# Expert gates of two dense blocks: one-hot products, or indirect additions into a zeroed DRAM tensor

## The chip, the cores and the metric

The kernel runs on one core of one Trainium2 chip, as one launch. Its metric is device time in microseconds, of three runs the median: 1672.23 (1667.02 to 1674.17). One further execution was taken by the hardware profiler; all rows of a profile here are from it. Engine names in rows: PE is TensorE, PEld its weight loads, DVE VectorE, ACT ScalarE, POOL GpSimd, SP SyncE, which issues nearly all plain transfers.

## The reference

One layer of a decoder trunk for 512 tokens of width 1024, fp32: a token-mixing half (attention over a window of 128, causal pooling, gated merge, residual), then PEER, a retrieval over 128 x 128 experts, then RMSNorm. The change lies in PEER, which per token is:

```python
q  = (xc @ w_query).reshape(c, 8, 2, 128)               # 8 heads, two halves
sc = einsum('chpd,hpkd->chpk', q, sub_keys)
sv, si = top_k(sc, 16)                                  # top 16 of 128 keys per half
cand = sv[:, :, 0, :, None] + sv[:, :, 1, None, :]      # 256 candidates
cidx = si[:, :, 0, :, None] * 128 + si[:, :, 1, None, :]
fv, fi = top_k(cand, 16);  idx = take_along_axis(cidx, fi)
g = softmax(fv)
a = gelu(einsum('chkd,cd->chk', u_tab[idx], xc))
out = einsum('chk,chkd->cd', g * a, v_tab[idx])         # 8 x 16 experts a token
```

Two heads of a token may choose the same expert, and then their gates add up; one head never chooses an expert twice.

## The kernel before

The 512 tokens are four blocks of 128. Block 0 goes ahead alone, with its tokens' experts fetched row by row from the tables (`gather`: 128 fetches of U rows and 128 of V rows, each an indirect transfer of GpSimd that brings one 4 KB row per token into one of five row buffers; VectorE multiplies by one instruction a fetch, L906 and L910). Blocks 1 to 3 are computed densely against all 16384 experts on the U side: 128 **U parts**, one per value of the expert's upper index i, each 24 matmuls of 128 x 128 by 384 columns (three products for split precision), whose Gelu gives, for the 128 lower indices j, the activations of the three blocks. Block 1's go to DRAM (`late`) and are picked from there one by one; those of blocks 2 and 3, 256 tokens, are kept in SBUF (`gk`, as many as `HELD` and `KEEP` allow) or written to DRAM (`ahead`) and reloaded. After the U parts comes the **dense stage**: for each i the activations are multiplied by a gate tile [j, token] (`mix`), split in two, and multiplied with the 128 V rows of that i (`v_mm`), while block 1's V rows are fetched by GpSimd (`gather_late`).

The gate tile is a dense matrix over experts and tokens with 128 nonzeros a token. Before, `onehot` makes it token by token: from the chosen experts' i, j and gates, transposed, ScalarE builds relu(g - g|j - j'|) (`absolute`, L746, and `build`, L752), VectorE the comparison of i (L755), TensorE one fp32 product of the two per token (L764, two instructions each), ScalarE copies eight tokens out of PSUM (L765), and SP writes 1 MB for each 16 tokens to `spill` (L767). `gate_tile` (L811) reads it back in four transfers of 256 KB for eight values of i, in runs of 512 B.

What sets the order: `run` (L941) issues parts one after another and between two of them spends a credit on a queue of background work. That queue is: choose the experts of block 2 (`select`, VectorE), of block 3, spread block 2, choose block 1, spread block 3, at a credit of `R_A` = 3.8 a part; beside it the fetches of block 0, at a rate that ends them four parts before the last. VectorE also splits each part's weights (L121), in its own program order between the products of fetched rows and the background's instructions. GpSimd does nothing here but issue indirect transfers, in order; a fetch waits for a free row buffer, which a product on VectorE frees.

Of the kernel before, what the change touches and what calls it, by code (L numbers as in the profile page):

```python
# [19 lines left out]
P = 128  # L20
# [26 lines left out]
TG = 16  # L47
NG = TD // TG
AJ = 4
NI = 8  # L50
# [4 lines left out]
HP = 400  # L55
U_S = 4
LOOK = 2
KEEP = 4
HELD = (42, 50)
# [4 lines left out]
class Layer:  # L64
    def __init__(self, ctx, tc, a):
        self.ctx, self.tc, self.nc, self.a = ctx, tc, tc.nc, a
        nc = self.nc
        self.c = self.pool("const", 1)
        self.s = self.pool("small", 2)
        self.w = self.pool("wstream", 2)  # L70
        self.rows = self.pool("rows", ROWS, side="right", reuse_waits="tile")
        self.work, self.owed = [], 0.0
# [17 lines left out]
        self.spill = nc.dram_tensor("spill", (NG, P, NKEY, TG), F32, kind="Internal").ap()  # L90

    def consts(self):
# [6 lines left out]
        self.tok = self.c.tile([P, 1], I32, name="tok")  # L99
# [522 lines left out]
    def scores(self, xn2, tp, sv, si, subk):  # L622
# [23 lines left out]
        for i in range(16):  # L646
# [10 lines left out]
            yield  # L657
        match(i, last)
# [60 lines left out]
    def indices(self, tp, ei):  # L719
        v = self.nc.vector  # L720
        ij = tp.tile([P, 2, P], I32, name="ij", tag="ij", bufs=1)
        v.tensor_scalar(ij[:, 0, :], ei, 7, None, op0=ALU.arith_shift_right)
        v.tensor_scalar(ij[:, 1, :], ei, NKEY - 1, None, op0=ALU.bitwise_and)
        jf = tp.tile([P, 2, P], F32, name="jf", tag="jf", bufs=2)
        v.tensor_copy(jf[:, 0, :], ij[:, 0, :])
        v.tensor_scalar(jf[:, 1, :], ij[:, 1, :], -1.0, None, op0=ALU.mult)
        return jf

    def onehot(self, tp, c, jf, g):
        nc = self.nc  # L730
        v = nc.vector
        ps = self.mm_tile(3 * P)
        for n, src in enumerate((jf[:, 0, :], jf[:, 1, :], g)):
            nc.tensor.transpose(ps[:, n * P:(n + 1) * P], src, self.ident)
        yield 2
        tr = tp.tile([P, 4, P], F32, name="tr3", tag="tr3", bufs=1)
        v.tensor_copy(tr[:, :3, :].rearrange("p a b -> p (a b)"), ps)
        v.tensor_scalar(tr[:, 3, :], ps[:, 2 * P:], -1.0, None, op0=ALU.mult)
        iob = self.iota.unsqueeze(1).to_broadcast([P, 8, P])
        gs = {}  # L740

        def absolute(n):
            u = 8 * n
            ohj = tp.tile([P, 8, P], F32, name="ohj", tag="k4", bufs=4)
            for z in range(8):
                nc.scalar.activation(ohj[:, z, :], self.iota, AF.Abs, bias=tr[:, 1, u + z:u + z + 1])  # L746
            return ohj

        def build(n, ohj):
            u = 8 * n  # L750
            for z in range(8):
                nc.scalar.activation(ohj[:, z, :], ohj[:, z, :], AF.Relu, bias=tr[:, 2, u + z:u + z + 1],  # L752
                                     scale=tr[:, 3, u + z:u + z + 1])
            ohi = tp.tile([P, 8, P], F32, name="ohi", tag="k4", bufs=4)
            v.tensor_tensor(ohi, iob, tr[:, 0, u:u + 8].unsqueeze(2).to_broadcast([P, 8, P]), op=ALU.is_equal)  # L755
            return ohj, ohi

        def product(n, ohj, ohi):
            t0 = 8 * n % TG
            if t0 == 0:  # L760
                gs[0] = tp.tile([P, NKEY, TG], F32, name="gs", tag="gs", bufs=2)
            pg = self.big([P, 8, P], "pg")
            for z in range(8):
                nc.tensor.matmul(pg[:, z, :], lhsT=ohj[:, z, :], rhs=ohi[:, z, :], start=True, stop=True)  # L764
            nc.scalar.copy(gs[0][:, :, t0:t0 + 8].rearrange("p i t -> p t i"), pg)  # L765
            if t0 + 8 == TG:
                nc.sync.dma_start(out=self.spill[(c * P + 8 * n) // TG], in_=gs[0])  # L767

        last = None
        for n in range(P // 8):  # L770
            ohj = absolute(n)
            yield 2.4
            new = build(n, ohj)
            yield 3.2
            if last:
                product(n - 1, *last)
                yield 1.9
            last = new
        product(n, *last)
# [26 lines left out]
    def gate_tile(self, n, q, parts=4):  # L806
        b = n // NI
        if q == 0:
            self.gts[b] = self.dp.tile([P, NG, NI, TG], F32, name="gt", tag="gt", bufs=2)
        s = slice(q * NG // parts, (q + 1) * NG // parts)  # L810
        self.nc.sync.dma_start(out=self.gts[b][:, s].rearrange("p g i t -> p g (i t)"),  # L811
                               in_=self.spill[s, :, n:n + NI, :].rearrange("g p i t -> p g (i t)"))

# [8 lines left out]
    def mix(self, m):  # L822
        nc, dp, gts = self.nc, self.dp, self.gts
        ga = self.reload(m)
        if 0 < m % NI < 5 and m - m % NI + NI < NKEY:
            self.gate_tile(m - m % NI + NI, m % NI - 1)
# [3 lines left out]
        nc.vector.tensor_tensor(wf.rearrange("p (g t) -> p g t", t=TG), ga.rearrange("p (g t) -> p g t", t=TG),  # L830
                                gts[m // NI][:, :, m % NI, :], op=ALU.mult)
# [39 lines left out]
    def rows_of(self, tab, ei, s):  # L871
        t = self.rows.tile([P, D], F32, name="row", tag="row")
        self.nc.gpsimd.indirect_dma_start(out=t, out_offset=None, in_=tab,  # L873
                                          in_offset=bass.IndirectOffsetOnAxis(ap=ei[:, s:s + 1], axis=0))
        return t

    def gather_late(self, ei, ea, g, z):
# [3 lines left out]
        def elem(s):  # L881
            nc.gpsimd.indirect_dma_start(out=act[:, s:s + 1], out_offset=None, in_=self.late,  # L882
                                         in_offset=bass.IndirectOffsetOnAxis(ap=ea[:, s:s + 1], axis=0))
# [57 lines left out]
    def run(self):  # L941
# [12 lines left out]
        with tc.tile_pool(name="route", bufs=1, side="right", reuse_waits="tile") as tp:  # L954

            def pool(b):
                return self.ga if b == LB else tp

# [3 lines left out]
            def wide(shape):  # L962
                return tp.tile(shape, F32, name="eq", tag="k4", bufs=4)
# [4 lines left out]
            ei = {b: pool(b).tile([P, P], I32, name=f"ei{b}", bufs=1) for b in late_blocks}  # L968
            gw = {b: pool(b).tile([P, P], F32, name=f"gw{b}", bufs=1) for b in late_blocks}
            ea = self.ga.tile([P, P], I32, name="ea", bufs=1)  # L970

            jf = {}

            def choose(b):
                yield from self.select(small, wide, sv[b], si[b], ei[b], gw[b])
                if b >= VB:
                    jf[b] = self.indices(tp, ei[b])
                else:
                    nc.vector.tensor_scalar(ea, ei[b], 7, None, op0=ALU.logical_shift_left)
                    nc.vector.tensor_tensor(ea, ea, self.tok.to_broadcast([P, P]), op=ALU.bitwise_or)  # L980
                yield 1

            def spread(b):
                yield from self.onehot(tp, b - VB, jf[b], gw[b])
# [20 lines left out]
            bg = Background(choose(2), choose(3), spread(2), choose(LB), spread(3))  # L1005
            rate = (2 * PH * TOPK - fetch.spent) / (NKEY - ahead - 4)
            while not bg.done:
                after = part()
                with tc.issue_after(after):
                    bg.spend(R_A)  # L1010
                    fetch.spend(rate)
        self.home, self.room = self.pool("more", 1, reuse_waits="tile"), HELD[1]
        while ahead < NKEY:
            with tc.issue_after(part()):
                fetch.spend(rate)
        fetch.spend(1e9)
        self.xs.close()
        with tc.tile_pool(name="dense", bufs=2, reuse_waits="tile") as self.dp:
# [7 lines left out]
            late = Background(self.gather_late(ei[LB], ea, gw[LB], h1))  # L1026
# [34 lines left out]

def blocks(w):
# [42 lines left out]
```

## Time and profile before

| | us |
|---|---|
| runs, median (lowest to highest) | 1672.23 (1667.02 to 1674.17) |
| the profiled execution | 1678.03 |
| its span, first to last instruction | 1676.0 |
| TensorE busy, and share | 1515.9, 90% |
| VectorE | 1276.3, 76% |
| ScalarE | 835.7, 50% |
| GpSimd | 668.8, 40% |
| mean granted TensorE clock | 0.961 |

The span is what the trace shows; the profiled execution's own time lies 2 us above it. Shares are means over stages that differ: mixing and block 0 up to about 500 us, scores of blocks 1 to 3 up to about 600, U parts up to 1200, the dense stage after that. A matmul's length in a row is that of its passage through a pipeline; matmuls start closer to each other than they are long, so the pace of TensorE is read from their count in a stretch. A GpSimd row with DMA_INDIRECT is the time GpSimd needs to issue the transfer, not the transfer's.

### The profile page before, as it was taken

To read this page: it belongs to the slowest core of one execution; us is meant where nothing else is said; L and a number is where in the kernel's file an instruction comes from. 1 tells how busy PE (TensorE), PEld (TensorE's weight loads), DVE (VectorE), ACT (ScalarE), POOL (GpSimd) and SP (SyncE) were. 2 spreads that over 40 slices of the span, in tenths; PEclk is the share of its full clock that TensorE was granted. 3 is DMA by queue.
4 is the path that set the end of the run, shared out by engine and by line. 5 is a ranking of instruction groups with operands and counts; after the bars stand their busy time and mean duration, and the time that the engine had idled before them with its cause. 6 is when DMAs were issued, how large, how long until landed. Compare 5 with 4: busy or idle time off the path is not lost.

```text
span 1676.0 us, 23878 instructions
## 1 busy us (share of the span) xinstructions
PE 1515.9 (90%) x8234; PEld 1356.9 (81%) x8234; DVE 1276.3 (76%) x2395; ACT 835.7 (50%) x1663; POOL 668.8 (40%) x518
## 2 busy tenths in 40 slices
PE   6898979999779989789999999999789898888887
PEld 5797967899679979789999999999766665666665
DVE  2402878889857999977789876677379898898898
ACT  4411346643234333399994999833334343333344
POOL 0000010255520024544435544354277776676730
PEclk9998989999889999989999999999899999999999
DMA  7685242499973348789999999998689999999995
GB/s 270 229 296 206 70 162 94 161 349 341 363 263 105 129 157 295 258 289 344 334 356 316 381 354 345 360 323 313 188 278 357 357 343 369 358 376 372 347 358 206
DMA packets 189465, 476.41 MB, mean 284 GB/s; under 512 B 21408, under 2 KB 84896, under 8 KB 187040
## 3 DMA queue, kind: packets, MB, share of 16 engines
q1 hardware_dynamic: 128736, 270.31, 45.5%
q0 software_dynamic: 59392, 201.42, 34.1%
q10 hardware_dynamic: 1216, 3.15, 0.6%
q8 instruction: 65, 1.06, 0.3%
q14 instruction: 56, 0.46, 0.1%
HBM read 438.50 MB, written 35.78 MB: 283 GB/s over the span
## 4 chain that ended last, share of the span: by engine, by line
PE 28%; DMA 10%; ACT 9%; DVE 7%; issue 4%; POOL 1%; DVEq 0%; ACTq 0%; POOLq 0%
DMA wr<-v_experts 8%; PE mm L116 6%; PE mm L117 6%; PE mm L118 6%; DVE wl L121 4%; PE acc L117 4%; PE acc L118 3%; PE acc L116 3%; ACT wh L127 2%; ACT ohj L752 2%; ACT ohj L746 2%; PE pg L764 2%; ACT gs L765 1%; POOL act L882 1%; DVE h L895 1%
## 5 line engine op out<-in xcount | busy, mean ns | idle before, releaser
L121 DVE TENSOR_TENSOR wl<-wr,wh 128x1024 fp32r<-128x1024 f32 x315 | 385.5, 1225 | 199.0 <-ACT wh L127 196.7
L116 PE MATMUL mm<-xh,wh 128*128 128x384 f32 (+1 forms) x1408 | 486.3, 346 | 19.1 <-ACT gk L795 16.6
L127 ACT CAST wh<-wr 128x1024 fp32r<-128x1024 f32 x315 | 331.9, 1054 | 331.6 <-PE mm L117 239.0
L118 PE MATMUL mm<-xh,wl 128*128 128x384 f32 (+1 forms) x1408 | 479.7, 341 | 7.3 <-DVE wl L121 7.3
L117 PE MATMUL mm<-xl,wh 128*128 128x384 f32 (+1 forms) x1408 | 479.0, 340 | 5.6 <-DVE xl L121 5.6
L873 POOL DMA_INDIRECT row<-u_experts,eig x128 | 196.8, 1537 | 602.6 <-DVE hg L910 250.7
L116 PEld LDWEIGHTS mm<-xh,wh 128*128 128x128 f32 x1408 | 267.8, 190 | 27.1 <-ACT gk L795 19.4
L118 PEld LDWEIGHTS mm<-xh,wl 128*128 128x128 f32 x1408 | 267.7, 190 | 8.8 <-DVE wl L121 8.8
L117 PEld LDWEIGHTS mm<-xl,wh 128*128 128x128 f32 x1408 | 267.7, 190 | 6.0 <-DVE xl L121 5.8
L117 PE MATMUL acc<-wl,wh 128*128 128x512 f32 x512 | 220.3, 430 | 33.3 <-DVE wl L121 30.8
L873 POOL DMA_INDIRECT row<-v_experts,eig x128 | 174.6, 1364 | 187.0 <-DVE row L906 130.9
L116 PE MATMUL acc<-wh 128*128 128x512 f32 x512 | 210.6, 411 | 27.3 <-ACT wh L127 17.8
L118 PE MATMUL acc<-wh,wl 128*128 128x512 f32 x512 | 208.6, 407 | 0.0
L873 POOL DMA_INDIRECT row<-v_experts,ei x128 | 146.6, 1145 | 101.6 <-DVE h L895 76.0
L882 POOL DMA_INDIRECT act<-late,ea x128 | 150.1, 1173 | 80.2 <-DMA late<-a 41.5
L117 PEld LDWEIGHTS acc<-wl,wh 128*128 128x128 f32 x512 | 101.2, 198 | 95.3 <-DVE wl L121 76.2
L832 ACT CAST wh<-wf 128x256 fp32r<-128x256 f32 x128 | 52.1, 407 | 241.2 <-DVE wf L830 201.1
L906 DVE SCALAR_TENSOR_TENSOR row<-row,natg 128x1024 f32<-128x1024 f32 x128 | 155.8, 1221 | 18.4 <-DMA row<-u_experts,eig 18.3
L895 DVE SCALAR_TENSOR_TENSOR h<-row,act,h 128x1024 f32<-128x1024 f32 x128 | 163.9, 1280 | 4.4 <-DMA row<-v_experts,ei 3.7
L910 DVE SCALAR_TENSOR_TENSOR hg<-row,act,hg 128x1024 f32<-128x1024 f32 x128 | 164.1, 1282 | 3.3 <-DMA row<-v_experts,eig 2.7
L116 PEld LDWEIGHTS acc<-wh 128*128 128x128 f32 x512 | 100.9, 197 | 58.5 <-ACT wh L127 26.1
L118 PEld LDWEIGHTS acc<-wh,wl 128*128 128x128 f32 x512 | 101.1, 198 | 18.6
(245 smaller groups left out, 1850.9 us busy)
## 6 DMA issues: line engine op xcount, KB each, us to landing
wr<-u_blocks SPq DMA_DIRECT2D x128, 512.0 KB, 5.8
wr<-v_experts SPq DMA_DIRECT2D x128, 512.0 KB, 6.5
spill<-gs SPq DMA_DIRECT2D x16, 1024.0 KB, 8.9
gt<-spill SPq DMA_DIRECT2D x64, 256.0 KB, 8.1
row<-w_in SPq DMA_DIRECT2D x30, 512.0 KB, 4.3
wr<-w_in SPq DMA_DIRECT2D x30, 512.0 KB, 3.8
row<-w_query SPq DMA_DIRECT2D x16, 512.0 KB, 4.3
wr<-w_query SPq DMA_DIRECT2D x16, 512.0 KB, 3.4
```

The source lines that it names most:

```text
L116: mm(out, lhsT=l[0], rhs=r[0], start=first, stop=False)
L117: mm(out, lhsT=l[0], rhs=r[1], start=False, stop=False)
L118: mm(out, lhsT=l[1], rhs=r[0], start=False, stop=last)
L121: self.lowered = self.nc.vector.tensor_tensor(lo, src, hi.bitcast(F32), op=ALU.subtract).ins
L127: self.nc.scalar.copy(hi, raw)
L746: nc.scalar.activation(ohj[:, z, :], self.iota, AF.Abs, bias=tr[:, 1, u + z:u + z + 1])
L832: nc.scalar.copy(wh, wf)
L873: self.nc.gpsimd.indirect_dma_start(out=t, out_offset=None, in_=tab, in_offset=bass.IndirectOffsetOnAxis(ap=ei[:, s:s + 1], axis=0))
L882: nc.gpsimd.indirect_dma_start(out=act[:, s:s + 1], out_offset=None, in_=self.late, in_offset=bass.IndirectOffsetOnAxis(ap=ea[:, s:s + 1], ...
L895: nc.vector.scalar_tensor_tensor(z, v, act[:, s:s + 1], z, op0=ALU.mult, op1=ALU.add)
L906: nc.vector.scalar_tensor_tensor(u, u, 1.0, xn, op0=ALU.mult, op1=ALU.mult, accum_out=act[:, s:s + 1])
L910: nc.vector.scalar_tensor_tensor(z, v, act[:, s:s + 1], z, op0=ALU.mult, op1=ALU.add)
```

## The change

`onehot`, `indices` and the DRAM tensor `spill` go. A DRAM tensor `gate` of 128 x 128 x 256 floats (16 MB, index [i, j, token]) is filled with zeros by 16 transfers of 1 MB from a zeroed tile, issued by SP between the query projections of `scores`. Each chosen expert's place is computed on VectorE (`ea`: expert number shifted left by 8, or'ed with the token's number), and GpSimd adds the gates there by indirect transfers with an addition: one transfer for each head and rank, 128 tokens each, 256 transfers in all. As two heads can name the same place, a head's first transfer waits until all 16 of the same block's head before it have landed; within a head the places differ. `Turns` alternates between blocks 2 and 3 after each head. All fetches and scatters are held in program order on GpSimd (`queued`).

The background's order changes with it: first block 2's choice alone, at `R_A` and without fetches; then blocks 3 and 1 at `R_B` = 1.5 a part, with fetches and `R_S` = 2.4 scatters a part; after that the scatters left are spread evenly up to four parts before the last. Gate tiles are for four values of i instead of eight, one transfer of 128 KB per i in runs of 1 KB. 96 activation tiles are held instead of 75.

```diff
-HELD = (42, 50)
+HELD = (64, 28)
...
+            if i == 0:
+                zero = tp.tile([P, D * 2], F32, name="zero", bufs=1)
+                nc.vector.memset(zero, 0.0)
+                blank = self.gate.rearrange("(a p f) o -> a p (f o)", p=P, f=D * 2)
+            nc.sync.dma_start(out=blank[i], in_=zero)
...
+    def scatter(self, c, ea, g):
+        sync, order = (mybir.DependencyInfo(k, mybir.DependencyReason.DATA)
+                       for k in (mybir.DependencyClass.Sync, mybir.DependencyClass.NoSync))
+        last = []
+        for h in range(PH):
+            now = []
+            for k in range(TOPK):
+                s = h * TOPK + k
+                ins = self.nc.gpsimd.indirect_dma_start(
+                    out=self.parts[c * TOPK + k], out_offset=bass.IndirectOffsetOnAxis(ap=ea[:, s:s + 1], axis=0),
+                    in_=g[:, s:s + 1], in_offset=None, compute_op=ALU.add).ins
+                for p in now[:1] if now else last:
+                    self.tc.add_manual_dep(ins, p.name, order if now else sync, reason="one head after the other")
+                now.append(ins)
+                self.queued(ins)
+                yield 1
+            last = now
...
-            self.gts[b] = self.dp.tile([P, NG, NI, TG], F32, name="gt", tag="gt", bufs=2)
-        s = slice(q * NG // parts, (q + 1) * NG // parts)
-        self.nc.sync.dma_start(out=self.gts[b][:, s].rearrange("p g i t -> p g (i t)"),
-                               in_=self.spill[s, :, n:n + NI, :].rearrange("g p i t -> p g (i t)"))
+            self.gts[b] = self.dp.tile([P, NI, TD], F32, name="gt", tag="gt", bufs=2)
+        s = slice(q * NI // parts, (q + 1) * NI // parts)
+        self.nc.sync.dma_start(out=self.gts[b][:, s],
+                               in_=self.gate.rearrange("(n p t) o -> p n (t o)", p=P, t=TD)[:, n + s.start:n + s.stop])
...
+                nc.vector.tensor_scalar(ea[b], ei[b], 7 if b == LB else 8, None, op0=ALU.logical_shift_left)
+                nc.vector.tensor_tensor(ea[b], ea[b], self.tok[:, c:c + 1].to_broadcast([P, P]), op=ALU.bitwise_or)
                 if b >= VB:
-                    jf[b] = self.indices(tp, ei[b])
...
+                    spread.queue.append(self.scatter(c, ea[b], gw[b]))
...
-            bg = Background(choose(2), choose(3), spread(2), choose(LB), spread(3))
-            rate = (2 * PH * TOPK - fetch.spent) / (NKEY - ahead - 4)
+            first, bg = Background(choose(2)), Background(choose(3), choose(LB))
             while not bg.done:
                 after = part()
                 with tc.issue_after(after):
-                    bg.spend(R_A)
-                    fetch.spend(rate)
+                    if not first.done:
+                        first.spend(R_A)
+                        rate = (2 * PH * TOPK - fetch.spent) / (NKEY - ahead - 4)
+                    else:
+                        bg.spend(R_B)
+                        fetch.spend(rate)
+                        spread.spend(R_S)
         self.home, self.room = self.pool("more", 1, reuse_waits="tile"), HELD[1]
+        late = (NV * PH * TOPK - spread.spent) / (NKEY - ahead - 4)
         while ahead < NKEY:
             with tc.issue_after(part()):
                 fetch.spend(rate)
+                spread.spend(late)
+        spread.spend(1e9)
         fetch.spend(1e9)
...
+class Turns(Background):
+    def spend(self, amount):
+        self.credit = min(self.credit + amount, 1e9)
+        while self.credit > 0 and self.queue:
+            cost = next(self.queue[0], None)
+            if cost is None:
+                self.queue.pop(0)
+                continue
+            self.credit -= cost
+            self.spent += cost
+            if self.spent % TOPK == 0:
+                self.queue.append(self.queue.pop(0))
```

On GpSimd before, in the U stage, block 0's fetches stand alone, V and U rows in turn:

```order
L873 DMA row<-v_experts,eig 128x1024
L873 DMA row<-u_experts,eig 128x1024
L873 DMA row<-v_experts,eig 128x1024
L873 DMA row<-u_experts,eig 128x1024
L873 DMA row<-v_experts,eig 128x1024
```

Now, at the same place (gw_3870 and ea_3873 are block 2's gates and places):

```order
L841 DMA row<-u_experts,eig 128x1024
L841 DMA row<-v_experts,eig 128x1024
L734 DMA gate<-gw_3870,ea_3873 4194304x1 x2
L841 DMA row<-u_experts,eig 128x1024
L841 DMA row<-v_experts,eig 128x1024
L734 DMA gate<-gw_3870,ea_3873 4194304x1 x3
L841 DMA row<-u_experts,eig 128x1024
L734 DMA gate<-gw_3870,ea_3873 4194304x1 x2
```

75 of the 256 fetches stand ahead of the first scatter; the other 181 stand among the 256 scatters, two or three scatters after every one or two fetches. Block 2's first four heads stand in a row, then heads of blocks 3 and 2 in turn, then block 3's last four in a row.

On VectorE before, where block 3 is spread (L121 is the weight split of a part, L906 and L910 the products of fetched rows, L755 a comparison for the one-hot matrices):

```order
L121 TENSOR_TENSOR wl<-wr,wh 128x1024
L910 SCALAR_TENSOR_TENSOR hg<-row,act,hg 128x1024
L755 TENSOR_TENSOR ohi<-iota,tr_8258 128x1024
L121 TENSOR_TENSOR wl<-wr,wh 128x1024
L906 SCALAR_TENSOR_TENSOR row,act<-row,natg 128x1024
L910 SCALAR_TENSOR_TENSOR hg<-row,act,hg 128x1024
```

Now, in the second half of the U parts (the same three are L123, L875 and L879):

```order
L123 TENSOR_TENSOR wl<-wr,wh 128x1024
L875 SCALAR_TENSOR_TENSOR row,act<-row,natg 128x1024
L879 SCALAR_TENSOR_TENSOR hg<-row,act,hg 128x1024
L123 TENSOR_TENSOR wl<-wr,wh 128x1024
L879 SCALAR_TENSOR_TENSOR hg<-row,act,hg 128x1024
L875 SCALAR_TENSOR_TENSOR row,act<-row,natg 128x1024
```

The comparisons are gone and the splits still stand behind products of fetched rows. After the last such product, five splits are left.

## Rows read from the trace of the kernel before

**Rows 1.** The page: busy time by engine; DMA share in 40 slices of 41.9 us.

```profile
PE 1515.9 (90%) x8234; PEld 1356.9 (81%) x8234; DVE 1276.3 (76%) x2395; ACT 835.7 (50%) x1663; POOL 668.8 (40%) x518
...
DMA  7685242499973348789999999998689999999995
```

**Rows 2.** Stretches: length, busy (instructions) of PE, PEld, DVE, ACT, POOL; clock; DMA share, GB/s.

```profile
599.80:648.90 49.10, 44.66 (x245) 44.02 (x244) 49.10 (x141) 17.73 (x33) 18.14 (x10) 0.97 0.63 208
648.90:707.00 58.10, 50.01 (x270) 48.44 (x269) 58.00 (x154) 19.33 (x36) 32.99 (x17) 0.97 0.81 280
...
725.00:854.00 129.00, 125.67 (x766) 125.38 (x765) 91.28 (x100) 126.01 (x296) 59.34 (x43) 0.96 0.92 333
...
914.70:1080.00 165.30, 165.02 (x1030) 164.72 (x1029) 121.74 (x135) 160.82 (x370) 77.49 (x54) 1.00 0.98 360
1080.00:1161.00 81.00, 81.00 (x460) 81.00 (x459) 58.08 (x56) 28.57 (x58) 40.38 (x28) 1.00 0.95 333
...
1203.80:1232.00 28.20, 22.29 (x84) 17.04 (x85) 14.21 (x23) 9.85 (x15) 22.09 (x21) 0.82 0.71 214
1232.00:1398.00 166.00, 145.87 (x551) 106.71 (x550) 146.43 (x192) 63.12 (x92) 123.16 (x105) 0.94 1.00 355
1398.00:1611.00 213.00, 186.53 (x702) 134.06 (x700) 186.38 (x243) 81.30 (x117) 140.93 (x121) 0.95 1.02 361
```

**Rows 3.** The same view, of instructions on tile mm alone.

```profile
1100.00:1150.00 50.00, 50.00 (x285) 50.00 (x284) 0.00 (x0) 5.99 (x22) 1.00 0.96 336
```

**Rows 4.** Timelines (start, length): block 2's gates done; the last U part's Gelu.

```profile
648.86 0.29 DVE L716 TENSOR_TENSOR gw<-gw,gden 128x128 f32<-128x128 f32 x1
...
1200.31 0.38 ACT L795 ACTIVATE gk<-mm 128x256 f32<-128x256 f32 x1
```

**Rows 5.** Groups by line: count, busy us, mean ns, idle before, and its releasers.

```profile
L873 POOL DMA_INDIRECT row<-u_experts,eig x128 | 196.8, 1537 | 602.6 <-DVE hg L910 250.7 <-DVE sk L714 214.5 <-DVE row L906 121.4
...
L882 POOL DMA_INDIRECT act<-late,ea x128 | 150.1, 1173 | 80.2 <-DMA late<-a 41.5 <-issue 36.9 <-DMA row<-v_experts,ei 1.2
```

**Rows 6.** GpSimd's timeline: start, length, instruction, idle before it and releaser.

```profile
672.10 5.26 POOL L873 DMA_INDIRECT row<-u_experts,eig  x1 [0.66 <-DVE ff L694]
...
1161.34 0.94 POOL L873 DMA_INDIRECT row<-v_experts,eig  x1 [0.65 <-DVE hg L910]
1203.81 0.94 POOL L882 DMA_INDIRECT act<-late,ea  x1 [41.53 <-DMA late<-a]
1205.06 0.95 POOL L882 DMA_INDIRECT act<-late,ea  x1 [0.30 <-issue]
```

**Rows 7.** Groups by line, of the one-hot gates.

```profile
L752 ACT ACTIVATE ohj<-ohj,tr 128x128 f32<-128x128 f32 x256 | 107.3, 524 | 0.0
...
L746 ACT ACTIVATE ohj<-iota,tr 128x128 f32<-128x128 f32 x256 | 80.0, 427 | 7.0 <-DVE tr L737 7.0
L764 PE MATMUL pg<-ohi,ohj 128*128 128x128 f32 x512 | 65.1, 280 | 2.9 <-ACT ohj L752 2.9
L765 ACT COPY gs<-pg 128x1024 f32<-128x1024 f32 x32 | 64.8, 2030 | 1.7 <-PE pg L764 1.5
...
L755 DVE TENSOR_TENSOR ohi<-iota,tr 128x1024 f32<-128x1024 f32 x32 | 39.1, 1221 | 0.0
```

**Rows 8.** Groups by line, VectorE's weight splits and row products.

```profile
L121 DVE TENSOR_TENSOR wl<-wr,wh 128x1024 fp32r<-128x1024 f32 x315 | 385.5, 1225 | 199.0 <-ACT wh L127 196.7
...
L910 DVE SCALAR_TENSOR_TENSOR hg<-row,act,hg 128x1024 f32<-128x1024 f32 x128 | 164.1, 1282 | 3.3 <-DMA row<-v_experts,eig 2.7
...
L906 DVE SCALAR_TENSOR_TENSOR row<-row,natg 128x1024 f32<-128x1024 f32 x128 | 155.8, 1221 | 18.4 <-DMA row<-u_experts,eig 18.3
```

**Rows 9.** DMA issues: count, KB each, median us from issue to landing.

```profile
gar<-ahead SPq DMA_DIRECT2D x53, 128.0 KB, 8.5
...
row<-u_experts,eig POOLq DMA_INDIRECT x128, 7.3
...
act<-late,ea POOLq DMA_INDIRECT x128, 6.4
```

More of the change, by code (lines that the diff above doesn't have):

```diff
@@ L8 @@
 from concourse import mybir
+from concourse.bass_types import dram_disjoint_views
 from concourse.bass_utils import run_bass_kernel_spmd
@@ L46 @@
 TD = NV * P
-TG = 16
-NG = TD // TG
+NZ = 16
 AJ = 4
-NI = 8
+NI = 4
 R_A = 3.8
@@ L55 @@
 HP = 400
+R_S, R_B = 2.4, 1.5
 U_S = 4
@@ L71, in __init__ @@
         self.rows = self.pool("rows", ROWS, side="right", reuse_waits="tile")
-        self.work, self.owed = [], 0.0
+        self.work, self.before = [], None
         self.xs = ExitStack()
@@ L89, in __init__ @@
         self.late = nc.dram_tensor("late", (NKEY * P * P, 1), F32, kind="Internal").ap()
-        self.spill = nc.dram_tensor("spill", (NG, P, NKEY, TG), F32, kind="Internal").ap()
+        self.gate = nc.dram_tensor("gate", (NKEY * P * TD, 1), F32, kind="Internal").ap()
+        self.parts = dram_disjoint_views(self.gate, NV * TOPK)
     def consts(self):
@@ L98, in consts @@
         self.iota = self.const("iota", a["iota"].partition_broadcast(P), [P, P])
-        self.tok = self.c.tile([P, 1], I32, name="tok")
+        self.tok = self.c.tile([P, NV], I32, name="tok")
         self.nc.sync.dma_start(out=self.tok, in_=a["tok"])
@@ L717, in select @@
         yield SC
[L719 to L779, printed above, removed]
@@ L781, in u_part, with queued @@
+    def queued(self, ins):
+        if self.before is not None:
+            info = mybir.DependencyInfo(mybir.DependencyClass.NoSync, mybir.DependencyReason.DATA)
+            self.tc.add_manual_dep(ins, self.before.name, info, reason="fetches and scatters in program order")
+        self.before = ins
     def u_part(self, n, w, xn2):
@@ L824, in mix @@
         ga = self.reload(m)
-        if 0 < m % NI < 5 and m - m % NI + NI < NKEY:
-            self.gate_tile(m - m % NI + NI, m % NI - 1)
+        if m - m % NI + NI < NKEY:
+            self.gate_tile(m - m % NI + NI, m % NI)
         wf, wh, wl = (dp.tile([P, TD], t, name="w" + k, tag="wf" + k)
@@ L829, in mix @@
         yield
[L830 to L831 removed]
+        nc.vector.tensor_tensor(wf, ga, gts[m // NI][:, m % NI], op=ALU.mult)
         nc.scalar.copy(wh, wf)
@@ L872, in rows_of @@
         t = self.rows.tile([P, D], F32, name="row", tag="row")
-        self.nc.gpsimd.indirect_dma_start(out=t, out_offset=None, in_=tab,
-                                          in_offset=bass.IndirectOffsetOnAxis(ap=ei[:, s:s + 1], axis=0))
+        self.queued(self.nc.gpsimd.indirect_dma_start(
+            out=t, out_offset=None, in_=tab, in_offset=bass.IndirectOffsetOnAxis(ap=ei[:, s:s + 1], axis=0)).ins)
         return t
@@ L881, in elem @@
         def elem(s):
-            nc.gpsimd.indirect_dma_start(out=act[:, s:s + 1], out_offset=None, in_=self.late,
-                                         in_offset=bass.IndirectOffsetOnAxis(ap=ea[:, s:s + 1], axis=0))
+            self.queued(nc.gpsimd.indirect_dma_start(
+                out=act[:, s:s + 1], out_offset=None, in_=self.late,
+                in_offset=bass.IndirectOffsetOnAxis(ap=ea[:, s:s + 1], axis=0)).ins)
         for k in range(TOPK):
@@ L954, in run @@
         with tc.tile_pool(name="route", bufs=1, side="right", reuse_waits="tile") as tp:
-            def pool(b):
-                return self.ga if b == LB else tp
             def small(n, shape, dt=F32):
@@ L962, in wide @@
             def wide(shape):
-                return tp.tile(shape, F32, name="eq", tag="k4", bufs=4)
+                return tp.tile(shape, F32, name="eq", tag="k4", bufs=3)
             late_blocks = range(LB, NBLK)
@@ L967, in run @@
             si = {b: tp.tile([P, 16, TOPK], U32, name=f"si{b}") for b in late_blocks}
[L968 to L972, printed above, removed]
+            ei, gw, ea = ({b: self.ga.tile([P, P], t, name=f"{n}{b}", bufs=1) for b in late_blocks}
+                          for n, t in (("ei", I32), ("gw", F32), ("ea", I32)))
+            spread = Turns()
             def choose(b):
                 yield from self.select(small, wide, sv[b], si[b], ei[b], gw[b])
+                c = max(b - VB, 0)
+                nc.vector.tensor_scalar(ea[b], ei[b], 7 if b == LB else 8, None, op0=ALU.logical_shift_left)
+                nc.vector.tensor_tensor(ea[b], ea[b], self.tok[:, c:c + 1].to_broadcast([P, P]), op=ALU.bitwise_or)
                 if b >= VB:
-                    jf[b] = self.indices(tp, ei[b])
-                else:
-                    nc.vector.tensor_scalar(ea, ei[b], 7, None, op0=ALU.logical_shift_left)
-                    nc.vector.tensor_tensor(ea, ea, self.tok.to_broadcast([P, P]), op=ALU.bitwise_or)
+                    spread.queue.append(self.scatter(c, ea[b], gw[b]))
                 yield 1
-            def spread(b):
-                yield from self.onehot(tp, b - VB, jf[b], gw[b])
             ahead = 0
@@ L1025, in run @@
             mix = self.open_dense()
-            late = Background(self.gather_late(ei[LB], ea, gw[LB], h1))
+            late = Background(self.gather_late(ei[LB], ea[LB], gw[LB], h1))
             late.spend(0.01)
@@ L1059, in spend @@
                 self.spent += cost
+class Turns(Background):
[10 more added lines that the diff above has]
+                self.queue.append(self.queue.pop(0))
+        if not self.queue:
+            self.credit = min(self.credit, 0)
 def blocks(w):
@@ L1093 @@
         "iota": np.arange(P, dtype=f),
-        "tok": np.arange(P, dtype=np.int32)[:, None],
+        "tok": np.arange(P, dtype=np.int32)[:, None] + P * np.arange(NV, dtype=np.int32)[None, :],
         "fewpos": np.concatenate([np.arange(off, off + na * n) for _, na, n, off, _ in FEW]).astype(f),
```

## Prediction

> **What bounds the kernel now.** I read the page's busy line first: TensorE is busy 90% of the span and GpSimd 40% [rows 1]. Such averages hide the stages, so the table by stretches came next [rows 2], cut where the work changes: the reader should look down the TensorE column and, beside it, at the VectorE, ScalarE and GpSimd columns. From 600 to 1200 us the kernel computes the 128 U parts (24 matmuls of 384 columns each). Three regimes follow each other there. While a block's experts are chosen, VectorE is full (49.10 of 49.10, 58.00 of 58.10 us) and TensorE has holes. While one-hot gates are built (725 to 854 and 915 to 1080), TensorE and ScalarE are both full. From 1080 TensorE alone is full. There a 50 us stretch holds 285 of the 384-column matmuls [rows 3], so an undisturbed part is 24 x 50/285 = 4.21 us. The last U part's Gelu stands at 1200.3 [rows 4]. Then the V part runs to the end with the DMA engines at shares of 1.00 and more [rows 2].
>
> The third thing to see is GpSimd. Its share of 40% looks like room, but an indirect transfer holds GpSimd about a microsecond whatever its size. Two of its groups show it: 1537 ns for a gather of 128 rows of 4 KB beside a busy VectorE, 1173 ns for a gather of 128 single elements [rows 5]. Where these stand back to back, 0.30 us of "issue" lies between two of them [rows 6]. The cycle is thus 0.94 + 0.30 = 1.25 us where VectorE leaves it alone.
>
> **What goes.** 512 matmul instructions into pg (65.1 us busy; they lie in the TensorE-full stretches), 512 activations of ScalarE (107.3 + 80.0 us), 32 copies of 2030 ns (64.8), 32 VectorE comparisons (39.1) [rows 7], and 16 spills of 1 MB. If nothing else became late, the U stage would be TensorE's again: parts of 4.21 us instead of (1200.3 - 648.9)/113 = 4.88. The ScalarE work is worth nothing by itself, as TensorE is full beside it.
>
> **What comes.** On GpSimd, 256 scatters (2 blocks x 8 heads x 16). Its order shows 75 of the 256 row fetches of block 0 ahead of the first scatter, so 181 fetches and 256 scatters, 437 instructions, have to pass one in-order queue after block 2's experts are chosen and before the dense stage may read its first gate. The new gates wait for all of them; the fetches wait too, since each is queued between scatters, and VectorE's weight splits (L121) stand behind the row products in VectorE's order, so TensorE waits for GpSimd in the end.
>
> Start. Block 2 is chosen at 648.9 [rows 4]. The changed loop fetches no rows before that, which takes 10 fetches [rows 2] and their row products (1.2 to 1.3 us each, L906 and L910 [rows 8]) out of a full VectorE stretch; TensorE's 245 matmuls there need 245 x 50/285 = 43 of the 49 us. So 6 us earlier, unless the 16 MB of zeros get in the way: the same bytes as the spill, but now in the score stage. At the 360 GB/s of a full stretch [rows 2] that is 47 us of the DMA engines, in a stage of 16 query projections and four U parts, 20 x 4.21 = 84 us up to 600, where they are 30 to 40% busy [rows 1]. It fits, barely, if spread; I cost it at 4 us (0 to 15; its cover is the weights read three blocks ahead). Start 647.
>
> Cycle. No accumulating scatter stands in this trace. The nearest row is the element gather: as many descriptors, the same 4-byte elements. From 1204 to 1232, VectorE busy 14.21 of 28.20 us, 21 such instructions took 22.09 us, 1.05 each; from 1232 to 1398, VectorE busy 146.43 of 166.00, 105 took 123.16, 1.17 each [rows 2]. With the 0.30 between them: 1.35 at half load, 1.47 at 88%. VectorE's load in the changed U stage: 113 splits x 1.225 = 138, 181 row products x 1.25 (L906 1221, L910 1282 ns [rows 8]) = 226, and two choices of about 22 us (58.0 in the stretch from 649 to 707, less 11 splits and 17 products [rows 2, 8]), together 409 of some 660 us, 62%. Between the two points that is 1.39; a choice's instructions hold GpSimd longer (one fetch took 5.26 us [rows 6]), so 1.42. Bounds: 1.25 from below, as the shortest indirect rows have it, and 1.54 + 0.30 = 1.84 from above, by the dearest group [rows 5]. 437 x 1.42 = 620 us, 5.49 a part. TensorE, busy three quarters of it, may be granted less clock: 0.82 stands in the stretch to 1232, at 22.29 busy of 28.20 us [rows 2]. A part would then take 4.21/0.82 = 5.1, which GpSimd still covers.
>
> The Trainium skill, "DMA: Bandwidth & Descriptors" (Anatomy of one DMA, SWDGE path), puts most of a software DMA's fixed cost of some 2 us into completion, and only some 50 ns of dispatch and a small descriptor generation before it; by that the queue would pass 437 transfers almost for nothing, and the first rival below would hold. The trace disagrees: 0.94 us of GpSimd for each. The same page (SWDGE vs HWDGE vs iDMA) says that the descriptor rings lie in SBUF that VectorE locks GpSimd out of in its two-port modes; the cycle's rise with VectorE's load agrees.
>
> Waits between heads. A head's first scatter waits until all of the same block's head before have landed. In GpSimd's order the heads of blocks 2 and 3 alternate in the middle, but four heads of block 2 open the row and four of block 3 close it: 3 + 3 waits. An element gather lands 6.4 us after its issue [rows 9]; two or three instructions stand between, so about 3.5 each, 20 us (0 to 60).
>
> Tail. After the last fetch it takes 7.3 us to land [rows 9]; by VectorE's order five weight splits stand behind its product, 5 x 4.21 us of TensorE, and three scatters overlap: 25 us (before, 39 lay between the last fetch at 1161.3 and the last part [rows 6, 4]).
>
> End of the U stage: 647 + 620 + 20 + 25 = 1312, where it was 1200: **+112 us**.
>
> Dense stage. 96 U results are held in SBUF instead of 75, so 32 are reloaded instead of 53 [rows 9]: 21 x 128 KB at 361 GB/s is 7.6 us of a DMA-full stage; the first gate tile is 0.5 MB instead of 1 MB, 1.5 us. The gates' runs grow from 512 B to 1 KB, which I leave at nothing (0 to 10 us; no row separates them). -9 (0 to -20), for GpSimd's own chain there, 256 x 1.47 = 376 us, and VectorE at 88% cap what faster DMA can give.
>
> Sum: +112 - 9 = +103. The profiled execution took 1678.03 us, 1676.0 of it span; so 1781 for such a one. It lies 5.8 above the runs' median, and 1672 + 103 gives **1775 us**.
>
> **Rivals.**
> A, faster: a scatter holds GpSimd for less than any gather here, and TensorE bounds again. For: it moves only 4 bytes per descriptor. Against: so does the element gather, and no indirect row is under 0.93. Break-even, with the rest as above, is at (620 - 103)/437 = 1.18 us mean, which with fetches at 1.42 means scatters at (517 - 257)/256 = 1.02, 0.72 busy. At 0.8 the stage ends at 647 + 113 x 4.21 + 5 = 1128: -72 - 9, 1591 us. Chance 0.13, most of it short of that, near 1630.
> B, about no change: every instruction at the 1.25 floor, waits between heads hidden, dense gain whole: 647 + 546 + 25 = 1218, +18 - 20, 1670. For: VectorE is slower to interfere when TensorE is slow. Against: VectorE's 62% load. Chance 0.07.
> C, far slower: the accumulating scatter needs more of GpSimd than a gather, as it must read its target as well, or lands late. At the bound of 1.84, and fetches at 1.42, 471 + 257 = 728, with 25 more for waits the stage ends at 1445: +245 - 9, 1908. It decides from about 1.65 a scatter, where the time passes 1830. Chance 0.18.
> The forecast, GpSimd bound with mean cycles from 1.3 to 1.55, 1720 to 1830: chance 0.62.
>
> **How the numbers follow.** Measurement cannot tell less than 0.5%, about 8 us, from none. Faster is A, 0.13; same is B, 0.07; slower is the forecast and C, 0.80. The range must leave out at most 0.2: it takes B whole and the near edge of A, and goes into C as far as scatters of 1.75: 1655 to 1860.
>
> **What would show it.** GpSimd busy 80% or more of 650 to 1300 with "issue" as the idle time before its instructions; TensorE's U parts every 5.5 to 6 us, its idle time put down to VectorE's splits, and VectorE's to the DMA of rows; no time on L746 to L765; the last Gelu of a U part near 1310. A scatter row well under 0.8 us busy would prove me wrong, and so would a U stage with parts of 4.2 us and GpSimd still idle between fetches. If the scatter's mean is 1.1 but the heads' waits exceed 10 us each, the place is right and the price is not.

## The result and the profile after

The changed kernel takes 1929.22 us (median of four runs, 1922.46 to 1939.71) where the kernel before takes 1673.2: a ratio of 1.154, 95% interval 1.148 to 1.160. 1775 was forecast, with a range up to 1860. It is slower, as forecast, and GpSimd bounds it, as forecast; the size is off by 154 us.

The page of the profiled execution (1937.9 us span) answers to [rows 1]. First busy time, then the 40 slices (48.4 us each) of TensorE, GpSimd and the granted clock:

```profile
PE 1548.9 (80%) x7716; PEld 1369.6 (71%) x7716; DVE 1244.6 (64%) x2356; ACT 608.1 (31%) x1119; POOL 1088.8 (56%) x774
...
PE   6989799977998766676776766676667899989987
...
POOL 0000102554000878888888888888883777878740
PEclk9999899988999888787988888888887999999998
```

ScalarE and TensorE have lost their one-hot work [rows 7] and only idle longer. GpSimd runs at seven to eight tenths from the 14th slice to the 30th, its gaps of 0.30 us between instructions counted as idle.

The stretches answer to [rows 2]: length, busy (instructions) of PE, PEld, DVE, ACT, POOL, clock, DMA share, GB/s. The first two are the U stage from the first scatter to the last, the others the opening of the dense stage and its run:

```profile
629.20:1043.00 413.80, 289.69 (x1314) 277.25 (x1313) 221.57 (x417) 87.89 (x174) 341.08 (x216) 0.84 0.69 188
1043.00:1456.00 413.00, 284.81 (x1329) 272.68 (x1329) 180.54 (x189) 80.77 (x165) 340.84 (x221) 0.87 0.77 208
1482.50:1510.00 27.50, 19.75 (x73) 15.17 (x73) 13.89 (x22) 8.89 (x15) 17.18 (x16) 0.81 0.69 224
1510.00:1900.00 390.00, 348.52 (x1356) 251.34 (x1355) 360.90 (x472) 155.28 (x226) 286.84 (x240) 0.97 1.00 368
```

216 + 221 are the 437 instructions that were counted. They are busy 681.9 of 826.8 us; 437 gaps of 0.30 make 131 more. That leaves 14 us in which GpSimd waited for anything. TensorE is granted 0.84 to 0.87 of full speed there, a mean over its two levels of 1.2 and 2.4 GHz, and is busy 70% of the stretch with gaps at each part, where before it was full at 1.00; its 115 U parts left at 629 come every (1482.5 - 629.2)/115 = 7.4 us, where one of 4.21 us at full clock would take 5.0 at 0.84 (an estimate), so nothing depends on it.

GpSimd's groups answer to [rows 5]; its timeline shows two scatters and two fetches:

```profile
L734 POOL DMA_INDIRECT gate<-gw,ea x256 | 451.1, 1762 | 250.4 <-DVE ea L942 160.5 <-issue 76.7 <-DMA gate<-gw,ea 9.7
L841 POOL DMA_INDIRECT row<-u_experts,eig x128 | 168.4, 1316 | 380.4 <-DVE sk L721 213.2 <-DVE row L875 112.5 <-DVE hg L879 26.1
```

```profile
638.84 1.60 POOL L734 DMA_INDIRECT gate<-gw,ea  x1 [0.30 <-issue]
640.74 1.58 POOL L734 DMA_INDIRECT gate<-gw,ea  x1 [0.30 <-issue]
642.62 1.01 POOL L841 DMA_INDIRECT row<-u_experts,eig  x1 [0.31 <-issue]
643.94 1.05 POOL L841 DMA_INDIRECT row<-v_experts,eig  x1 [0.30 <-issue]
```

Beside fetches of about 1.0 us the scatters stand at 1.6. The mean is 1762 ns. The 160.5 us on ea are the time before the first scatter; waits for another head's landing (releaser gate) are 9.7 us in all.

The waits, of the whole execution, show who waited in turn: engine and line, for whom, us in total, times, longest.

```profile
ACT wh L129 <- PE mm L119: 492.2, 114, 11.8
PEld mm L120 <- DVE wl L123: 243.0, 75, 7.2
DVE hg L879 <- DMA row<-v_experts,eig: 236.1, 83, 7.8
...
DVE row L875 <- DMA row<-u_experts,eig: 202.7, 76, 7.6
```

This is the chain that the prediction named: VectorE waits 439 us for rows that GpSimd issued late (423 of them between 600 and 1490), and TensorE waits for the weight splits that stand behind those products. Following TensorE's own wait alone, one would have found VectorE, and VectorE is busy half of the stretch; only its wait leads on to GpSimd.

### The profile page after: what moved, and what is told of

It reads as the page before. It is cut to its first block, busy times and chain, and to the rows that moved or that the text cites. A ratio compares the mean times of both kernels' runs of the same rounds, so it can differ in the third digit from the quotient of the medians.

```text
span 1937.9 us, 22570 instructions
## 1 busy us (share of the span) xinstructions
PE 1548.9 (80%) x7716; PEld 1369.6 (71%) x7716; DVE 1244.6 (64%) x2356; ACT 608.1 (31%) x1119; POOL 1088.8 (56%) x774
## 5 line engine op out<-in xcount | busy, mean ns | idle before, releaser
L120 PE MATMUL mm<-xh,wl 128*128 128x384 f32 (+1 forms) x1408 | 523.4, 372 | 219.4 <-DVE wl L123 219.4
L734 POOL DMA_INDIRECT gate<-gw,ea x256 | 451.1, 1762 | 250.4 <-DVE ea L942 160.5
L118 PE MATMUL mm<-xh,wh 128*128 128x384 f32 (+1 forms) x1408 | 520.2, 370 | 49.0 <-ACT gk L764 38.9
L119 PE MATMUL mm<-xl,wh 128*128 128x384 f32 (+1 forms) x1408 | 512.3, 364 | 5.4 <-DVE xl L123 5.4
L120 PEld LDWEIGHTS mm<-xh,wl 128*128 128x128 f32 x1408 | 296.3, 210 | 243.1 <-DVE wl L123 243.0
L123 DVE TENSOR_TENSOR wl<-wr,wh 128x1024 fp32r<-128x1024 f32 x315 | 384.4, 1221 | 66.0 <-ACT wh L129 65.2
L841 POOL DMA_INDIRECT row<-u_experts,eig x128 | 168.4, 1316 | 380.4 <-DVE sk L721 213.2
L118 PEld LDWEIGHTS mm<-xh,wh 128*128 128x128 f32 x1408 | 296.2, 210 | 57.0 <-ACT gk L764 41.4
L879 DVE SCALAR_TENSOR_TENSOR hg<-row,act,hg 128x1024 f32<-128x1024 f32 x128 | 164.5, 1285 | 236.4 <-DMA row<-v_experts,eig 236.1
L119 PEld LDWEIGHTS mm<-xl,wh 128*128 128x128 f32 x1408 | 295.7, 210 | 6.0 <-DVE xl L123 5.7
L875 DVE SCALAR_TENSOR_TENSOR row<-row,natg 128x1024 f32<-128x1024 f32 x128 | 156.0, 1222 | 202.8 <-DMA row<-u_experts,eig 202.7
L118 PE MATMUL acc<-wh 128*128 128x512 f32 x512 | 204.9, 400 | 13.7 <-ACT wh L800 7.9
L841 POOL DMA_INDIRECT row<-v_experts,eig x128 | 163.6, 1278 | 43.0 <-issue 25.0
```

What stands on the lines that cost most here:

```text
L118: mm(out, lhsT=l[0], rhs=r[0], start=first, stop=False)
L119: mm(out, lhsT=l[0], rhs=r[1], start=False, stop=False)
L120: mm(out, lhsT=l[1], rhs=r[0], start=False, stop=last)
L123: self.lowered = self.nc.vector.tensor_tensor(lo, src, hi.bitcast(F32), op=ALU.subtract).ins
L734: ins = self.nc.gpsimd.indirect_dma_start(out=self.parts[c * TOPK + k], out_offset=bass.IndirectOffsetOnAxis(ap=ea[:, s:s + 1], axis=0), i ...
L841: self.queued(self.nc.gpsimd.indirect_dma_start(out=t, out_offset=None, in_=tab, in_offset=bass.IndirectOffsetOnAxis(ap=ei[:, s:s + 1], ax ...
```

## Experiments

The theory after the result: 437 issues on GpSimd set the U stage, and an accumulating scatter costs it 0.6 us more than the gather from which it was priced. The rivals: the background's new order, the waits between heads and landings, or the scatter's direction. Spans and stages below are of one profiled execution each; runs of one kernel differ by about 1%. The chip that ran e1 to e4 took 1689.21 for its one run of the kernel before, so a difference of some 15 us between one of these and a run from elsewhere shows nothing; e1 to e4 share that chip, e5 to e8 another, e9 to e11 a third. "U end" is the last Gelu of a U part, "dense" what follows; both and the span are in us.

| kernel | span | U end | dense | scatters (or in their place), shortest, mean ns |
|---|---|---|---|---|
| before | 1676.0 | 1200.3 | 475.7 | none |
| changed | 1937.9 | 1482.5 | 455.4 | 256, 1541, 1762 |
| e1, no scatter | 1579.8 | 1116.7 | 463.0 | none |
| e2, plain scatter | 1816.6 | 1353.6 | 463.0 | 256, 957, 1184 |
| e3, gather | 1818.6 | 1353.1 | 465.4 | 256, 940, 1133 |
| e4, gather with addition | 1924.4 | 1464.2 | 460.1 | 256, 1529, 1734 |
| e5, half of the scatters | 1698.0 | 1240.4 | 457.6 | 128, 1562, 1995 |
| e6, 64 tokens each | 1895.1 | 1437.2 | 457.8 | 256, 1397, 1602 |
| e7, 75 tiles held | 1930.1 | 1472.9 | 457.2 | 256, 1541, 1737 |
| e8, half one-hot, half scatter | 1729.9 | 1252.3 | 477.6 | 128, 1554, 1958 |
| e9, reads in runs of 1 KB, 59 tiles held | 1681.0 | 1215.2 | 465.8 | none |
| e10, 59 tiles held | 1685.5 | 1208.2 | 477.3 | none |
| e11, e8 with plain scatter | 1668.3 | 1193.8 | 474.5 | 128, 963, 1344 |

**e1, no scatter.**

```diff
-                    spread.queue.append(self.scatter(c, ea[b], gw[b]))
+                    pass
```

> All else of the changed kernel, but no scatter is issued, so the gates of blocks 2 and 3 stay zero. Theory (GpSimd's issue of 256 scatters at 1.76 + 0.30 us sets the U stage): TensorE bounds the U parts again, 113 of 4.21 us from 629: they end near 1110 instead of 1482, and the span is about 1565. Rival (the new order of the background work, with choices and fetches at other rates, makes the stage long): the U stage stays over 1300 and the span over 1750.

Measured 1579.8, near the theory and far from the rival. From 640 to 1116 TensorE is full again and its clock is whole:

```profile
640.00:1116.00 476.00, 476.00 (x2696) 476.00 (x2695) 392.95 (x590) 177.91 (x353) 259.51 (x175) 1.00 0.94 344
```

The new order isn't what makes the stage long. All of the change but the scatters was worth 96 us against the kernel before, 84 of them in the U stage, where the one-hot work is gone, and 13 in the dense stage; the 256 scatters cost 358.

**e2, e3, e4: direction or addition.** The scatter's call in the changed kernel, and what stands in its place (`dump` is a part of the tile svg in SBUF):

```diff
 e2:
-                    in_=g[:, s:s + 1], in_offset=None, compute_op=ALU.add).ins
+                    in_=g[:, s:s + 1], in_offset=None).ins
 e3 (e4: the same, with compute_op=ALU.add):
-                    out=self.parts[c * TOPK + k], out_offset=bass.IndirectOffsetOnAxis(ap=ea[:, s:s + 1], axis=0),
-                    in_=g[:, s:s + 1], in_offset=None, compute_op=ALU.add).ins
+                    out=dump[:, s:s + 1], out_offset=None, in_=self.gate,
+                    in_offset=bass.IndirectOffsetOnAxis(ap=ea[:, s:s + 1], axis=0)).ins
```

> The 256 scatters write instead of adding (where two heads name one place, the sum is lost); queue, waits and order are as in the changed kernel. If the addition is what makes a scatter dearer than a gather (1.54 us at the shortest instead of 0.94): shortest about 0.94, mean about 1.2, U stage to about 1320, span about 1770. If the direction is (an index on the written side): 1.54 and 1.76 stay, span about 1938. If the waits between heads or the landing of additions set it: span between, with GpSimd idle.

> Each scatter is turned into a gather of the same 128 elements from the same DRAM tensor, at the same place of the queue and with the same waits between heads; the gates stay zero. Theory (only the price of the instruction was mis-sized): shortest 0.94 us, mean about 1.2, 437 instructions at about 1.5, U stage to about 1320, span about 1770, as the prediction had it. Rival (waits, or the slots of eight transfers in flight, hold the queue): span stays over 1880.

> As the run with gathers, but each adds its elements to what stands in SBUF. If the addition makes the instruction dear: shortest about 1.54 us, mean about 1.76, span about 1938. If the written side's index does: about 0.94 and 1.2, span about 1770.

The instruction's rows in e2, e3 and e4, shortest, median and longest in ns, first and last start:

```profile
L734 POOL DMA_INDIRECT gate<-gw,ea x256: 957/993/2796, 632.8 to 1325.7; - x128
```

```profile
L735 POOL DMA_INDIRECT svg<-gate,ea x256: 940/949/2767, 632.0 to 1324.8; - x128
```

```profile
L735 POOL DMA_INDIRECT svg<-gate,ea x256: 1529/1563/2583, 632.5 to 1437.6; - x128
```

The four corners separate cleanly. Direction adds 0.01 to 0.02 us to the shortest, the addition 0.58 to 0.59 either way. Spans follow: 1817 and 1819 without it, 1924 and 1938 with it. The waits between heads stand in all four, and GpSimd waits 8 to 10 us for the landings of a head in each, so they are not what sets it. e2 and e3 were expected at about 1770 and came 47 and 49 us later; e3 lies 40 us over the 1779 that the forecast's sum gives for such a span. Its GpSimd is busy 501.19 us for 437 instructions:

```profile
632.00:1325.00 693.00, 546.41 (x2640) 515.70 (x2640) 399.31 (x605) 169.35 (x339) 501.19 (x437) 0.85 0.73 236
```

That is 1.15 + 0.30 = 1.45 a cycle, against the 1.42 assumed; another 61 us (693 - 501 - 131) it waited, 8 of them for landings of a head and 51 for VectorE to free a row buffer:

```profile
POOL row L842 <- DVE row L876: 27.3, 5, 6.5
POOL row L842 <- DVE hg L880: 24.1, 6, 6.7
```

The forecast counted nothing for row buffers. With gathers at its price, its sum would thus have missed by 41 us of waits and 12 of cycle, against which stand 15 by which the queue began earlier.

**e5, half the scatters.**

```diff
-        for h in range(PH):
+        for h in range(PH // 2):
...
-R_S, R_B = 2.4, 1.5
+R_S, R_B = 1.2, 1.5
...
-        late = (NV * PH * TOPK - spread.spent) / (NKEY - ahead - 4)
+        late = (NV * PH * TOPK // 2 - spread.spent) / (NKEY - ahead - 4)
```

> Only heads 0 to 3 of blocks 2 and 3 are scattered (128 scatters with addition, spread at half the rate), so half of the gates are missing. Theory (GpSimd's sum sets the U stage: 128 x 2.06 + 181 x 1.56 = 546 us from 630): the stage ends near 1200, span about 1655. Rival (the time falls in proportion to what is left out between 1580 without and 1938 with all): 1759.

1698.0 lies between the two, 43 us over the theory. 309 instructions took from 628.2 to 1206.5 and were busy 482.19 us of it, which with 309 gaps leaves 4 us of waiting. GpSimd bounds still, but the scatter's mean rose to 1995 ns: with fewer scatters the rest runs faster, and VectorE is busy 68% of the stretch instead of 49% (402 of 827 us).

```profile
628.00:1207.00 579.00, 498.72 (x2607) 484.03 (x2606) 395.81 (x602) 167.43 (x336) 482.19 (x309) 0.94 0.91 279
```

So the price of a scatter isn't a constant: 1541 at the shortest, 1762 beside a VectorE at 49%, 1995 at 68%. The changed kernel's own trace says the same, scatter by scatter. The 79 scatters during which VectorE ran nothing took 1545 to 1616 ns, 1583 in the mean; the other 177 took 1842 in the mean, up to 2629. Two of its scatters, the first beside an idle VectorE, the second beside a row product and a split:

```profile
1446.08 1.57 POOL L734 DMA_INDIRECT gate<-gw,ea  x1 [0.30 <-issue]
1456.13 2.12 POOL L734 DMA_INDIRECT gate<-gw,ea  x1 [0.30 <-issue]
```

The Trainium skill, "DMA: Bandwidth & Descriptors" (SWDGE vs HWDGE vs iDMA), has the descriptor rings in SBUF that VectorE locks GpSimd out of in its two-port modes; the three means go the way it says, though no run here tells that mechanism from another contention of the two engines.

**e6, 64 tokens each.**

```diff
-out_offset=bass.IndirectOffsetOnAxis(ap=ea[:, s:s + 1], axis=0),
-                    in_=g[:, s:s + 1],
+out_offset=bass.IndirectOffsetOnAxis(ap=ea[:64, s:s + 1], axis=0),
+                    in_=g[:64, s:s + 1],
```

> All 256 scatters with addition, but each for the first 64 of the 128 tokens of its block; the other tokens' gates stay zero. If GpSimd's time goes with the descriptors, the shortest scatter falls from 1.54 to about 0.8 us and the span to about 1580 + (256 x 1.3 + 181 x 1.56 - 490) = 1705; if most of it is fixed, it stays over 1.3 and the span over 1860.

```profile
L734 POOL DMA_INDIRECT gate<-gw,ea x256: 1397/1454/2510, 632.2 to 1411.2; - x128
```

Half of the elements save 0.14 of 1.54 us, so by these two points, at 2.3 ns an element, some 1.25 us would be paid for the instruction whatever it moves (an estimate). The number of instructions is most of the cost, not the gates added.

**e7, 75 tiles held.**

```diff
-HELD = (64, 28)
+HELD = (64, 7)
```

> The changed kernel with 75 activation tiles held, as before the change, instead of 96. Theory (the 20 us that the dense stage gained come half from 21 reloads fewer, half from gate reads in longer runs): dense stage about 8 to 10 us longer than the changed kernel's 455, U stage unchanged by more than 5, span about 1946. Rival (the runs of 1 KB alone): dense stage unchanged.

The dense stage takes 457.2 us, where e5 and e6 on the same chip, with 96 tiles held, take 457.6 and 457.8: the theory is wrong, 21 reloads aren't felt in this kernel. That leaves the way in which the gates are read for what the dense stage gained.

**e8, half and half.** Made from the kernel before: block 2's gates are added into a zeroed 8 MB half in the old layout, block 3's built from one-hot matrices.

```diff
-            bg = Background(choose(2), choose(3), spread(2), choose(LB), spread(3))
+            first, bg = Background(choose(2)), Background(choose(3), spread(3), choose(LB))
...
+                        bg.spend(R_B)
+                        scat.spend(R_S)
```

> Half and half: the one-hot products make block 3's gates, 128 scatters with addition block 2's, into the layout of the kernel before, of which 8 MB are zeroed; fetches run from the start of the U parts. Theory: GpSimd has 165 x 1.56 + 128 x 2.06 = 521 us from about 649 and TensorE some 28 us less than before; the U stage ends between 1180 and 1215 and the time is 1655 to 1690, within 1% of before. Rival (the scatters hurt by more than GpSimd's queue, by memory traffic or by VectorE's contention): over 1720.

1729.55 us, ratio 1.032 (1.027 to 1.036): over the theory's 1655 to 1690 and in the rival's "over 1720". From the first scatter to the last fetch GpSimd is busy 456.71 of 561 us, and 294 gaps of 0.30 leave 16 of waiting, so its queue bounds, as in the theory; but scatters at a mean of 1958 ns, where 1762 was assumed, beside a VectorE at 69% explain 25 us, which is the contention that the rival named, and the stage began late, at 656.

```profile
656.00:1217.00 561.00, 492.28 (x2731) 479.52 (x2730) 386.00 (x586) 273.72 (x592) 456.71 (x294) 0.94 0.92 288
```

**e9, e10, e11.** e9 is the kernel before with `TG = 32` for 16, so that gates are read in runs of 1 KB, e10 its control; both hold 16 tiles fewer (`HELD = (26, 50)`). e11 is e8 with the scatter's `compute_op=ALU.add` left out.

> The kernel before (one-hot gates), with gates spilled by 32 tokens instead of 16, so that the dense stage reads them in runs of 1 KB instead of 512 B; the doubled staging tile costs 16 held activation tiles (59 held, 69 reloaded). Theory (the dense stage's 20 us came from the longer runs, since holding 96 or 75 tiles made no difference): dense stage 458 to 465 us instead of 476, time about 1658 (1645 to 1668). Rival (they came from something else in the changed kernel's gate reads, four values of i a tile, one transfer each): 1672 to 1685.

> The kernel before with 16 activation tiles fewer held and nothing else changed (59 held, 69 reloaded): the control for the run with longer runs. Theory (reloads are not felt, as 21 more were not): 1672, within 6 us. Rival (DMA bytes bound the dense stage, 16 x 128 KB at 361 GB/s): 1678.

> Half and half as before, but block 2's 128 scatters write instead of adding, so sums of two heads that name one place are lost. Theory (an addition costs GpSimd 0.58 us more wherever it stands): U stage ends 128 x 0.58 = 74 us earlier than the 1252 of the half and half with additions, unless TensorE binds first at about 1170; span 1650 to 1660. Rival (in that order GpSimd isn't what binds): span stays over 1710.

e9 took 1680.37 us, ratio 1.0035 (1.0014 to 1.0056), e10 1686.19, ratio 1.0065 (1.0035 to 1.0096). e9's time is thus the rival's and not the theory's. The dense stage is 465.8 us in e9, 477.3 in e10, by one trace each: runs of 1 KB are worth 11 of the 20 us. The DMA engines, full in both, move more there:

```profile
1275.00:1415.00 140.00, 119.87 (x462) 85.41 (x460) 123.66 (x162) 52.89 (x76) 108.13 (x89) 0.98 1.00 369
1415.00:1615.00 200.00, 176.21 (x683) 125.73 (x682) 180.87 (x236) 79.26 (x114) 140.77 (x119) 0.98 1.02 377
```

```profile
1268.00:1408.00 140.00, 118.94 (x444) 85.83 (x444) 119.53 (x157) 51.55 (x75) 102.42 (x87) 0.94 1.01 358
1408.00:1608.00 200.00, 171.52 (x656) 122.33 (x655) 173.76 (x226) 75.41 (x109) 138.87 (x118) 0.97 1.03 366
```

(The first two rows are e9's, the others e10's.) But the U stage ends at 1215 and 1208 instead of 1200, which eats the gain. In both, the first two products of gates, which in the kernel before follow the U parts at 1208.7, stand among the U parts, and VectorE waits there for the first gate tile. In e10:

```profile
1105.69 0.76 DVE L830 TENSOR_TENSOR wf<-gk,gt 128x256 f32<-128x256 f32 x2 [10.19 <-DMA gt<-spill]
```

From 1080 to 1161 TensorE is then busy 73 of 81 us in e10 and 72 in e9, where it was busy 81.00. So e10, whose theory of no change is wrong, is no clean control against the kernel before, and says nothing certain of reloads there; e9 and e10 share the hole and can be compared. The other 9 us of the dense gain stay open (tiles of four values of i, or one transfer for each, weren't tried alone).

e11 ends its U stage 58.5 us before e8, at 1193.8, with a mean of 1344 ns for 1958: the addition's price again, in another order. 74 us were expected, and the span of 1668.3 is 8 over what was; TensorE is busy 472.51 of the 506 us from 654 to 1160 and leaves little more to gain. None of e8 to e11 beats the kernel before beyond doubt.

## Why the prediction was wrong, by its steps

- **Which engine bounds: right.** 14 us of waiting in 827 on GpSimd. The waits came where the prediction put them, VectorE behind rows, TensorE behind splits.
- **The cycle: the step that failed.** "The nearest row is the element gather: as many descriptors, the same 4-byte elements", at 1.42 us with 1.84 as the upper bound. It is 1.762 + 0.30 = 2.06 for a scatter with addition, outside the bounds: 256 x 0.64 = 164 us. Even the scatters beside an idle VectorE, 1.58 + 0.30 = 1.88, are over the upper bound. The fetches came to (681.9 - 451.1)/181 + 0.30 = 1.58, 181 x 0.16 = 29 us more, though VectorE was busy 49% and not 62%; why they rose, no run separates. e3 puts the gather itself in the scatter's place and gets within 40 us of the forecast, so the step's size was wrong, not the mechanism; e4 shows that the addition is what was not priced. Both bounds were rows of gathers, and nothing in them held an addition. Rival C named the cause, "needs more of GpSimd than a gather", at 1908, with a chance of 0.18, and the range stopped short of it. Of its two reasons, late landing is refuted (4.0 us in the median, 9.7 us of waits); that the target must be read is not shown, as a gather that adds into SBUF (e4) costs as much and half the elements (e6) save only 0.14 us.
- **Start, waits, tail.** First scatter at 629.2 for 647. The forecast let TensorE's 245 matmuls limit what leaving out the fetches saves; but VectorE, full from 600 (29.20 of 29.20 us), set the choice's end, and only 13 U parts were done by then, where 17 had been at 648.9 (so that 111 parts and not 113 were left there, of 4.97 us and not 4.88). The zeros, issued from 484 to 543, cost nothing that can be seen: from 484 to 532 the DMA share is 0.94 and TensorE busy 48.00 of 48.00 us. Waits on GpSimd 14 us for 20: in e3, whose cycle is the forecast's, they were 61, so that this term came out is partly luck: beside the dearer scatters a row buffer was always free. Tail, from the last scatter, 1482.5 - 1456.1 = 26 for 25.
- The U stage: 1312 forecast, -18 + 164 + 29 - 6 + 1 = +170, which makes the 1482 measured.
- **Dense stage: -20 for -9**, at the bound given, in the profiled execution; e1 to e7, which read their gates the same way, have -10 to -19. Its reason was wrong: reloads, counted at 7.6 us, gave nothing (e7), and the runs of 1 KB, counted at nothing, gave 11 (e9 against e10).
- **Rival A** lost: no scatter held GpSimd under 1.54 us. Its time, 1591, is near that of e1, 1581.53, in which no scatter is issued at all. The Trainium skill ("DMA: Bandwidth & Descriptors", Anatomy of one DMA, SWDGE path) puts most of a transfer's fixed cost into completion and little into issue. Here a scatter lands 4.0 us (median) after its issue begins and holds GpSimd 1.76 of them, so the issue is not small; and in a queue of 437 the landings overlap, while GpSimd's times don't.

## What to carry to other kernels

Price a transfer by the engine that issues it: on GpSimd count the indirect instructions in the stage that must hold them, times their issue time, before counting bytes. Where an operation has a property that no row in the trace has (here the addition), the bound from above must leave room for that property, and a measurement of it by itself, one gather against one gather with addition, is worth more than any interpolation. Replacing 252 us of ScalarE's work and 65 of TensorE's by 528 us on an in-order queue that other work already uses needs that queue's spare time written out first.

## What was not expected of the hardware

- An indirect transfer that adds holds GpSimd 1.53 to 1.54 us at the shortest, one that doesn't 0.94 to 0.96, in either direction.
- With addition, 64 indices cost 1.40 and 128 cost 1.54 us.
- The same instruction's mean went from 1762 to 1995 ns with VectorE's load from 49 to 68%; beside an idle VectorE it was 1583.
- Reads of the same 16 MB in runs of 1 KB instead of 512 B were worth 11 us, by one trace each, in a stage where the DMA engines are full.
